# A two-layer trunk on one core: gate weights stacked as hi and lo, late constants moved, shift tiles in groups of four

## The chip, the core and the metric

The kernel runs on one core of a Trainium2 chip. Times are device microseconds of one execution; the time of a kernel is the median of its runs. The profile is of one further execution, recorded by the hardware profiler. PE is TensorE (PEld its weight loads), DVE VectorE, ACT ScalarE, POOL GpSimd, SP SyncE, whose queue issues most DMAs.

## The reference

One inference step of a two-layer trunk over 640 tokens (128 of context, 512 latent), width 2048, all in fp32. Each layer is an adaptive RMSNorm, an input projection, two mixers side by side, a SiLU gate, an output projection and a gated residual add. What the change touches is the modulation of the first layer and the low-rank gate of the linear attention:

```python
def modulation(cond, w, b):                    # cond: context vector, latent vector
    m = jax.nn.silu(cond) @ w + b              # w: 2048 x 6144
    return jnp.split(m, 3, axis=-1)            # shift, scale, gate

shift, scale, gate = modulation(c, ada_w[l], ada_b[l])
h = rms_norm(x, norm_g[l]) * (1.0 + scale) + shift
qa, ka, va, qb, kb, vb, rb, gp = split_cols(h @ w_in, EVEN_SPLITS)   # rb: 32 columns

r = rb.reshape(B, T, 2, GLA_RANK)              # gla_branch: two directions, rank 16
logit = jnp.einsum('btdr,drk->btdk', r, wg) + bg
g = jax.nn.log_sigmoid(logit) / GLA_NORMALIZER
```

## The kernel before

Tokens lie along the free dimension, features along the 128 partitions, so a projection's output chunk is 128 (or fewer) features by 640 tokens, made in two halves of 320 (322 with two extra columns, see below). Products in fp32 are made of rounded parts: every operand x is split into hi (rounded, by ScalarE) and lo = x - hi (by GpSimd), in the fast format fp32r, and a product is the sum of three matmuls, hi x hi, hi x lo, lo x hi (`mm_k`, recorded in `mm`, L393). `acth` and `actl` are the parts of the activations, `whi` and `wlo` those of the weights. A weight chunk is split in four units of 512 rows (4 slices of 128); the split weights lie in a ring of 2560 columns, the raw ones in four slots of `wraw`.

The order on the engines is fixed when the program is built: a planner (`Pace`) keeps its own clock for every engine and lets small tasks (generators, `tick`) fall in between the matmuls when its clock says that their inputs are there. Engines and queues then run in that order. So an edit at one place lays out anew the order of what follows.

**Start stage** (`start`). It makes the first layer's scale (16 tiles of 128 features) and shift (16 tiles) for two condition vectors, normalises x, and makes the first six weight chunks (`FIRST`) on the way: one over its whole depth ("lead") and five in windows of 2, 2, 4 and 8 slices, altogether 576 matmuls. A scale tile is a product of the condition vectors (`cond`, 32 columns, stationary) with 16 blocks of 128 x 128 of weights (`ada`, moving), four at a time side by side in the array, into four bands of 32 rows of one bank (L1360). ScalarE copies the bank out, one more matmul with `sel` adds the bands and turns the row into a column. The weights come in blocks of 512 KB on SyncE's queue into a ring of six (`NR`), two blocks to a tile; when a tile's matmuls are issued, its two slots are loaded anew.

Of the 16 shift tiles, eight (`BOTH`) are made in this way after the scale tiles. The other eight are sums on VectorE (`shifts`): rows of the transposed weights (`ada_s`, 256 KB a row quarter, five buffers `raw`) times a broadcast row of silu(c) (`crow_s`, from DRAM), a part of them offloaded to GpSimd and ScalarE (`prod`). When all are there, the shift is written into two extra columns of `acth` and `actl` (L1082, L1083), which later chunks carry along (322 columns), and TensorE transposes it (`tr`, L398) for a copy in DRAM.

At the very start, the loads are issued as follows: cT (the condition vectors) and then the weights on SyncE's queue; `small` (all small constants), the sink's logits and `crow` on ScalarE's. `crow` is passed through SiLU and written to DRAM as `crow_s`.

**The chunk behind the stage** is `w_rb`, the 32 columns of the gate's rank. Its raw weights are broadcast to three bands of 32 columns as they are split (M = 96), so that the result stands three times on 96 partitions, where `gla_rank` wants it as `r` (with the weights `wgs`, loaded from `gla_wgp`). It takes three products like any other chunk.

Of the kernel before, what the change touches and what calls it, by code (L numbers as in the profile page):

```python
# [19 lines left out]
KT = D // 128  # L20
# [27 lines left out]
BOTH = 8  # L48

# [168 lines left out]
class Core:  # L218
# [15 lines left out]
    ("gla_m1", 128),  # L234
    ("gla_mu", 128),
]


class Trunk:
# [9 lines left out]
    def __init__(self, tc, d, es):  # L249
# [29 lines left out]
        nc.sync.dma_start(self.cT, d["cT"])  # L279
        small = self.P([128, sum(w for _, w in SMALL)], "small")  # L280
        nc.scalar.dma_start(small, d["small"])
        at, c = 0, {}
        for name, w in SMALL:
            c[name] = small[:, at : at + w]
            at += w
# [6 lines left out]
        self.mu = c["gla_mu"].bitcast(U32)  # L292
        self.act(self.cT, self.cT, AF.Silu)
# [241 lines left out]
    def wstart(self, chunks, acts):  # L535
# [17 lines left out]
        self.both = {c for kind, x in acts if kind == "h" for c in x[:2]}  # L553
        seven = {c for kind, x in acts if kind == "s" for c in x}
        for kind, x in acts:
            if kind == "c" and x >= FIRST:
# [90 lines left out]
    def wpump(self, force=False):  # L647
# [113 lines left out]
    def units(self, c, k0, evac):  # L761

        p = []
        for k in range(k0, KT, 4):
# [10 lines left out]
            self.wdone((c, k, 0))  # L775

# [528 lines left out]
    def start(self):  # L1305
# [5 lines left out]
        with tc.tile_pool(name="su", bufs=1) as su:  # L1311
# [6 lines left out]
            rows = Ring([self.adas[:, 960 + 128 * i : 1088 + 128 * i] for i in range(3)])  # L1318
# [32 lines left out]
            def tiles():  # L1351
                for i in range(KT + BOTH):
                    ws = [ring[(2 * i + q) % NR].rearrange("p (a b) -> p a b", b=128) for q in range(2)]
                    yield from self.until(*ws)
                    self.now += 0.2
                    for j in range(16):
                        g = 32 * (j % 4)
                        o, c, w = pm[g : g + 32, 0:128], cond[:, j, :], ws[j // 8][:, j % 8, :]
                        self.pe(0.0575, o, c, w)
                        nc.tensor.matmul(o, c, w, start=j < 4, stop=j >= 12)  # L1360
                    self.now += 0.2
                    for q in range(2):
                        load(2 * i + q + NR)
                    yield
                    r = rows.next()
                    nc.scalar.activation(r, pm[:, 0:128], AF.Copy)
                    yield from self.until(r)
                    p = pcol.next()
                    self.mm(p, r, self.sel)
                    f = i if i < KT else i - BOTH  # L1370
                    x = self.adab[:, 0, f : f + 1]
                    if i >= KT:
                        nc.vector.tensor_scalar(self.sh0[:, :, f], p, x, None, ALU.add)
                        continue
                    x, g = self.b1[:, 0, f : f + 1], self.ng[:, 0, f : f + 1]
                    nc.vector.tensor_scalar(self.A[0][:, f, :], p, x, g, ALU.add, ALU.mult)
                    yield from self.wait(f"sq{f}")
                    self.act_mod(0, f, xs[f % NX], 0, T)
                    load_x(f + NX)
                    self.flags.add(f"act{f}")  # L1380
                self.flags.add("tiles")

            def shifts():
                raws = [self.t(su, [128, PIECE], "raw", bufs=self.NRAW) for _ in range(self.NRAW)]
                junk = self.adas[:, 1472 : 1472 + PIECE // 2].bitcast(BF16)
# [13 lines left out]

                for i in range(len(raws) - 1):  # L1400
# [84 lines left out]
            crow = self.adas[0:32, 1344:1472]  # L1485
# [8 lines left out]
            while lead or todo:  # L1494
# [11 lines left out]
                else:  # L1506
                    self.now += 0.2
            while self.tasks or self.low:
# [577 lines left out]
    def program(self):  # L2086
# [94 lines left out]
        add(d["w_rb"], 96, True, None, lazy("vt", rows=96, then=lambda x: self.spawn(self.gla_rank(x))))  # L2181
# [328 lines left out]
        with tc.manual_schedule():  # L2510
# [13 lines left out]
            for kind, x in acts:  # L2524
# [3 lines left out]
                elif kind == "s":  # L2528
                    self.spair(*x)
                elif kind == "k":  # L2530
# [105 lines left out]
def _consts():  # L2636
# [17 lines left out]
    return {"cos": c4, "sin": s4, "emask": em, "sel": sel, "gla_m1": m1, "gla_mu": mu}  # L2654
# [32 lines left out]
def _layout(i):  # L2687
# [20 lines left out]
    o["ada0"] = x.reshape(2, 8, 128, KT + BOTH, 128).transpose(3, 0, 2, 1, 4).reshape(-1, 128, 1024)  # L2708
# [29 lines left out]
    o["small"] = np.concatenate([o.pop(k).reshape(128, w) for k, w in SMALL], 1)  # L2738
# [37 lines left out]
```

## Time and profile before

| | |
|---|---|
| median of 3 runs | 2119.41 us (2116.44 to 2121.92) |
| profiled execution | 2118.93 us |
| its span, first to last instruction | 2117.1 us, granted TensorE clock 0.994 |
| TensorE busy | 2058.0 us (97%) |
| VectorE, ScalarE, GpSimd busy | 1320.0, 1071.2, 1285.1 us |
| moved by DMA | 341 MB, 161 GB/s over the span |
| start stage, to the first matmul of w_rb | 144.36 us |
| w_rb chunk | 144.36 to 158.48 us |

The span is that of the instructions; the profiled execution's own time is 1.8 us longer. A row of the timeline gives start, length, engine, line, operation, output and inputs, the shapes, how many instructions were merged, and in brackets the idle time before it with what ended it. An fp32 matmul leaves two records in the trace, an fp32r matmul one. Line numbers are those of the kernel before; L213 is the helper through which the vector engines' instructions go, L427 that of the DMAs on SyncE's queue.

### The profile page before, as it was taken

What the parts mean: (1) busy time and instruction counts of PE and PEld (TensorE: products, weight loads), DVE (VectorE), ACT (ScalarE), POOL (GpSimd) and SP (SyncE); (2) the same over time, 40 slices, a digit from 0 to 9 for tenths busy, and PEclk for the clock granted to TensorE, in tenths of its full rate; (3) what the DMA queues carried; (4) which work ended last, traced back from release to release, by engine and by line L of the source; (5) the groups of instructions that cost most, each with busy time, mean ns of one, the idle gap of its engine ahead of it and who ended that gap; (6) DMA issues with size and microseconds to landing.
All of it is one profiled execution on the core that took longest, in us unless ns stands there. A gap on an engine that the chain in (4) does not pass through costs nothing. (4 is left out here: it accounts for less than half of the span.)

```text
span 2117.1 us, 40263 instructions
## 1 busy us (share of the span) xinstructions
PE 2058.0 (97%) x14345; PEld 2003.7 (95%) x14345; DVE 1320.0 (62%) x3063; ACT 1071.2 (51%) x2471; POOL 1285.1 (61%) x1082
## 2 busy tenths in 40 slices
PE   7999999999999999999999999999999999999996
PEld 6899999999999999999999999999999999999995
DVE  4856686666556554988666878777454444465335
ACT  5645565454666665543564444444444544454433
POOL 4756564445545544888565656655555577668873
PEclk9999999999999999999999999999999999999998
DMA  9966343336464544576643455444322344354437
GB/s 363 398 226 189 121 158 107 111 119 197 130 206 150 150 136 145 187 229 219 213 130 105 136 160 159 143 139 149 94 81 90 108 139 130 124 202 132 128 95 248
DMA packets 193401, 341.23 MB, mean 161 GB/s; under 512 B 20944, under 2 KB 70192, under 8 KB 193200
## 3 DMA queue, kind: packets, MB, share of 16 engines
q1 hardware_dynamic: 191728, 337.10, 49.4%
q8 instruction: 112, 1.84, 0.4%
q10 hardware_dynamic: 1472, 1.56, 0.2%
q14 instruction: 89, 0.73, 0.1%
HBM read 304.08 MB, written 31.88 MB: 159 GB/s over the span
## 5 line engine op out<-in xcount | busy, mean ns | idle before, releaser
L393 PE MATMUL bank<-acth,whi 128*128 128x320 f32 (+2 forms) x3320 | 1021.5, 318 | 10.6 <-ACT bc L213 2.8
L393 PE MATMUL bank<-actl,whi 128*128 128x320 f32 (+2 forms) x3320 | 994.7, 310 | 3.7 <-DMA actl<-bl_dram 2.1
L393 PE MATMUL bank<-acth,wlo 128*128 128x320 f32 (+2 forms) x3320 | 994.5, 311 | 3.5 <-POOL wlo L213 3.5
L213 POOL TENSOR_TENSOR wlo<-wraw,whi 128x512 fp32r<-128x512 f32 (+1 forms) x452 | 573.6, 1281 | 412.1 <-ACT whi L213 329.8
L393 PEld LDWEIGHTS bank<-acth,whi 128*128 128x128 f32 (+1 forms) x3320 | 617.6, 189 | 20.9 <-ACT bc L213 3.9
L393 PEld LDWEIGHTS bank<-actl,whi 128*128 128x128 f32 (+1 forms) x3320 | 617.4, 189 | 6.9 <-DMA actl<-bl_dram 3.3
L393 PEld LDWEIGHTS bank<-acth,wlo 128*128 128x128 f32 (+1 forms) x3320 | 617.5, 189 | 5.1 <-POOL wlo L213 5.1
L213 POOL TENSOR_TENSOR wlo<-rs,whi 128x384 fp32r<-128x384 f32 x370 | 408.1, 1123 | 183.2 <-ACT whi L213 143.6
L213 ACT ACTIVATE whi<-wraw 128x512 fp32r<-128x512 f32 (+1 forms) x460 | 262.9, 588 | 93.2 <-PE bank L393 60.7
L393 PE MATMUL bank<-eh,wlo 128*128 128x322 f32 (+1 forms) x666 | 207.2, 311 | 2.7 <-POOL wlo L213 2.7
L393 PE MATMUL bank<-eh,whi 128*128 128x322 f32 (+1 forms) x666 | 209.3, 314 | 0.0
L393 PE MATMUL bank<-el,whi 128*128 128x322 f32 (+1 forms) x666 | 206.9, 311 | 0.0
L213 ACT ACTIVATE whi<-rs 128x384 fp32r<-128x384 f32 x370 | 182.0, 514 | 48.5 <-PE bank L393 41.7
L213 DVE TENSOR_TENSOR wraw<-rs 128x768 f32<-128x768 f32 x74 | 98.8, 1335 | 124.7 <-POOL wlo L213 69.9
L213 DVE CUSTOM_DVE_ANT_0 adas<-adas,bank,partg 128x256 bf16<-128x256 f32 (+1 forms) x290 | 156.2, 539 | 12.6 <-DMA adas<-ada_g 5.3
L213 POOL TENSOR_TENSOR prod<-adas,mixrow 128x512 f32<-128x512 f32 x85 | 111.5, 1321 | 70.4 <-ACT prod L213 48.5
L213 ACT ACTIVATE arena<-arena,bc 128x512 f32<-128x512 f32 (+4 forms) x211 | 106.4, 527 | 79.8 <-DVE arena L213 77.0
L393 PEld LDWEIGHTS bank<-eh,wlo 128*128 128x128 f32 x666 | 125.5, 189 | 3.9 <-POOL wlo L213 3.7
L393 PEld LDWEIGHTS bank<-eh,whi 128*128 128x128 f32 x666 | 125.7, 189 | 0.1
L393 PEld LDWEIGHTS bank<-el,whi 128*128 128x128 f32 x666 | 125.8, 189 | 0.0
L213 DVE CUSTOM_DVE_ANT_0 adas<-adas,bank,part 128x512 bf16<-128x512 f32 x151 | 112.4, 744 | 9.8 <-DMA adas<-ada 6.8
L213 ACT ACTIVATE arena<-Y 128x320 f32<-128x320 f32 (+1 forms) x76 | 38.9, 512 | 152.1 <-DVE Y L213 125.9
(218 smaller groups left out, 2480.1 us busy)
## 6 DMA issues: line engine op xcount, KB each, us to landing
wraw<-w_even SPq DMA_DIRECT2D x176, 256.0 KB, 3.4
adas<-ada_g SPq DMA_DIRECT2D x128, 256.0 KB, 3.7
adas<-ada SPq DMA_DIRECT2D x128, 256.0 KB, 3.8
rs<-w_odd SPq DMA_DIRECT2D x50, 384.0 KB, 3.3
wraw<-w_odd SPq DMA_DIRECT2D x74, 256.0 KB, 3.5
wraw<-w_out SPq DMA_DIRECT2D x64, 256.0 KB, 3.9
rs<-w_odd SPq DMA_DIRECT2D x50, 256.0 KB, 3.8
Y<-ada SPq DMA_DIRECT2D x24, 512.0 KB, 7.3
```

The lines of the kernel that those rows point to most:

```text
L213: return f(*args, **kw)
L393: self.nc.tensor.matmul(out, lhsT, rhs, start=start, stop=stop, **kw)
```

## The change

Three edits.

1. The chunk `w_rb` is split into one block of 64 columns, 32 of hi and 32 of lo, and a new function `quad` runs it: for each slice the block is multiplied by `acth` and by `actl` (two matmuls of 64 rows of output). The result is copied out of the bank by ScalarE into two buffers of `gt`; a task then multiplies it by a constant matrix `rep` (64 of 128 rows by 96 columns, fp32), which adds hi's and lo's parts and writes the sum to the three bands.
2. At the start: cT goes from SyncE's queue to ScalarE's, ahead of `small`. The constants `gla_m1`, `gla_mu` and the new `rep` leave `small` (420 columns, now 164) for a block `late` (352 columns), loaded at the end of the stage's matmuls together with the sink, on SyncE's queue. `crow` is loaded on SyncE's queue after the first scale tile, by a task of its own; `shifts` waits for it. The first tile's copy goes to VectorE.
3. The eight shift tiles on TensorE become two groups of four tiles: 16 matmuls of 512 columns for a group, in two batches of eight that each take four blocks of the ring; one copy by ScalarE, four matmuls with `sel`. The weights in DRAM are laid out accordingly; blocks and bytes stay the same.

In the changed program TensorE has 64 + 2 matmuls where w_rb had 96, and 32 of 512 columns where the shift tiles had 128 of 128.

```diff
+GROUPS = (*((f, 1) for f in range(KT)), *((f, 4) for f in range(KT, KT + BOTH, 4)))
...
-        nc.sync.dma_start(self.cT, d["cT"])
-        small = self.P([128, sum(w for _, w in SMALL)], "small")
-        nc.scalar.dma_start(small, d["small"])
+        nc.scalar.dma_start(self.cT, d["cT"])
+        for n, parts in (("small", SMALL), ("late", LATE)):
+            small, at = self.P([128, sum(w for _, w in parts)], n), 0
+            if n == "small":
+                nc.scalar.dma_start(small, d[n])
+            else:
+                self.late = small
...
-        if m < M:
-            raw = raw[:, :, None, :].to_broadcast([128, n, M // m, m])
-            hi, lo = (x.rearrange("p a (b c) -> p a b c", c=m) for x in hl)
+        if key[0] in self.stacked:
+            hl = hi
+            hi, lo = hl[:, :, :m], hl[:, :, m:]
...
+    def quad(self, c, parts):
+        _, M, shift, _, evac = self.chunks[c]
+        units = [(c, k, 0) for k in range(0, KT, 4)]
+        banks = [self.pj(), self.pj()]
+        for half, p in enumerate(banks):
+            cs = self.cols(half, shift)
+            n = cs.stop - cs.start
+            for u in units:
+                w = self.wget(u)
+                for j in range(4):
+                    for i, x in enumerate((self.ah, self.al)):
+                        k = u[1] + j
+                        self.mm(p[:M, :n], w[:, j, :], x[:, k, cs], start=k == i == 0, stop=k == KT - 1 and i == 1)
+                    if j % 2:
+                        self.tick()
+            self.nc.scalar.activation(parts[half][:M, :n], p[:M, :n], AF.Copy)
+            self.drop(p)
...
+        def work():
+            for half, x in enumerate(parts):
...
+                self.mm(p[:96, : x.shape[1]], self.rep[:M, :], x)
+                evac(*((None, p) if half else (p, None)))
...
             def tiles():
-                for i in range(KT + BOTH):
-                    ws = [ring[(2 * i + q) % NR].rearrange("p (a b) -> p a b", b=128) for q in range(2)]
+                at = 0
+                for i, n in GROUPS:
+                    m = 8 // n
+                    for b in range(0, 2 * n, 4):
+                        e = min(b + 4, 2 * n)
+                        ws = [ring[(at + q) % NR].rearrange("p (a b) -> p a b", b=128 * n) for q in range(e - b)]
+                        yield from self.until(*ws)
+                        for k in range(m * b, m * e):
+                            g = 32 * (k % 4)
+                            o, c, w = pm[g : g + 32, 0 : 128 * n], cond[:, k, :], ws[k // m - b][:, k % m, :]
+                            nc.tensor.matmul(o, c, w, start=k < 4, stop=k >= KT - 4)
+                        for q in range(e - b):
+                            load(at + q + NR)
+                        at += e - b
...
+                    if i == 0:
+                        nc.vector.tensor_copy(r, pm[:, : 128 * n])
+                    else:
+                        nc.scalar.activation(r, pm[:, : 128 * n], AF.Copy)
...
             def shifts():
...
+                yield from self.wait("crow")
...
-            nc.scalar.dma_start(self.sink, d["attn_sink"].partition_broadcast(128))
-            nc.scalar.dma_start(crow, d["crow"].rearrange("a (b c) -> (a b) c", c=128))
-            self.act(crow, crow, AF.Silu)
-            nc.scalar.dma_start(d["crow_s"].rearrange("a (b c) -> (a b) c", c=128), crow)
+            def rows0():
+                yield from self.wait("act0")
+                nc.sync.dma_start(crow, d["crow"].rearrange("a (b c) -> (a b) c", c=128))
+                yield 3.0
+                self.act(crow, crow, AF.Silu)
+                nc.scalar.dma_start(d["crow_s"].rearrange("a (b c) -> (a b) c", c=128), crow)
+                self.flags.add("crow")
+                yield
...
+            nc.sync.dma_start(self.late, d["late"])
+            nc.sync.dma_start(self.sink, d["attn_sink"].partition_broadcast(128))
...
-        add(d["w_rb"], 96, True, None, lazy("vt", rows=96, then=lambda x: self.spawn(self.gla_rank(x))))
+        add(d["w_rb"], 64, True, None, lazy("vt", rows=96, then=lambda x: self.spawn(self.gla_rank(x))))
+        acts.append(("q", acts.pop()[1]))
...
+    rep = np.tile(np.eye(32, dtype=f), (4, 3))
...
+    x = [x[:, :, f : f + n].reshape(2 * n, -1, 128, n * 128).transpose(0, 2, 1, 3) for f, n in GROUPS]
```

More of the change, by code (lines that the diff above doesn't have):

```diff
@@ L233 @@
     ("gmlp_gT", 8),
[L234 to L235 removed]
 ]
+LATE = [("gla_m1", 128), ("gla_mu", 128), ("rep", 96)]
 class Trunk:
@@ L775, in units @@
             self.wdone((c, k, 0))
+    def quad(self, c, parts):
[15 more added lines that the diff above has]
+            self.drop(p)
+        for u in units:
+            self.wdone(u)
+        def work():
+            for half, x in enumerate(parts):
+                cs = self.cols(half, shift)
+                x = x[:M, : cs.stop - cs.start]
+                yield from self.until(x)
+                yield from self.bank()
+                p = self.sm()
+                self.mm(p[:96, : x.shape[1]], self.rep[:M, :], x)
+                evac(*((None, p) if half else (p, None)))
+                yield
+        self.spawn(work(), first=True)
     @staticmethod
@@ L1317, in start @@
             sq, rt = self.adas[:, 0:T], self.adas[:, T : T + HT]
-            rows = Ring([self.adas[:, 960 + 128 * i : 1088 + 128 * i] for i in range(3)])
+            rows = Ring([self.adas[:, 960 + 512 * i : 1472 + 512 * i] for i in range(2)])
             NX, NR = 3, self.NRING
@@ L2529, in program @@
                     self.spair(*x)
+                elif kind == "q":
+                    self.quad(x, [L["gt"].next() for _ in range(2)])
                 elif kind == "k":
```

75 lines of the change are left out of this document (39 added, 36 removed).

## The prediction

> **What bounds the kernel now.** I read the page first, then busy time by stretches, then the timeline of the first 10 us and of 90 to 160 us, then the waits.
>
> ```profile
> span 2117.1 us, 40263 instructions
> PE 2058.0 (97%) x14345; PEld 2003.7 (95%) x14345; DVE 1320.0 (62%) x3063; ACT 1071.2 (51%) x2471; POOL 1285.1 (61%) x1082
> DMA  9966343336464544576643455444322344354437
> ```
> The profiled execution took 2118.93 us, 0.48 under the median of the runs (2119.41); 1.8 us of it lie outside the span. TensorE is busy nearly throughout, so a matmul less is time less, except where TensorE waits for data: the DMA row is full only in the first slices, that is in the start stage. The change is in that stage and in the chunk after it.
>
> ```profile
> 3.00:4.00 1.00, 0.00 (x0) 0.00 (x0) 0.30 (x1) 0.65 (x2) 0.46 (x5) 1.00 0.72 256
> 4.00:5.00 1.00, 0.00 (x0) 0.00 (x0) 0.32 (x1) 0.00 (x0) 0.29 (x4) 1.00 0.50 153
> 5.00:6.00 1.00, 0.00 (x0) 0.00 (x0) 0.00 (x0) 0.00 (x0) 0.00 (x0) 1.00 0.55 202
> ...
> 60.00:80.00 20.00, 20.00 (x259) 18.26 (x259) 16.82 (x29) 11.66 (x25) 16.59 (x12) 1.00 1.04 404
> 80.00:100.00 20.00, 19.22 (x242) 17.04 (x244) 15.93 (x33) 13.95 (x33) 10.17 (x8) 1.00 1.03 406
> 100.00:120.00 20.00, 18.02 (x237) 15.80 (x226) 10.55 (x30) 7.76 (x21) 11.95 (x10) 1.00 0.91 317
> 120.00:140.00 20.00, 20.00 (x139) 20.00 (x138) 16.84 (x50) 9.53 (x23) 14.33 (x12) 1.00 0.65 202
> 140.00:160.00 20.00, 20.00 (x139) 19.95 (x138) 6.44 (x19) 8.24 (x20) 10.89 (x12) 1.00 0.63 197
> ```
> Columns: length, busy time of PE, PEld, DVE, ACT, POOL, clock, DMA share, GB/s. From 60 to 100 us the transfers run at 405 GB/s, full, and TensorE is full as well: two bounds, side by side. From 3 to 6 us the transfers run at half that rate. From 120 us on TensorE is the only bound.
>
> ```profile
> 0.74 0.39 SPq L279 DMA_DIRECT2D cT<-cT  x1
> 1.18 0.45 ACTq L213 DMA_DIRECT2D sink<-attn_sink  x1
> 1.18 0.90 SPq L427 DMA_DIRECT2D Y<-ada  x2
> ...
> 3.44 0.23 ACT L213 ACTIVATE cT<-cT 128x32 f32<-128x32 f32 x1
> ...
> 3.54 0.29 POOL L213 TENSOR_SCALAR b<-small 128x32 f32<-128x32 f32 x1 [2.13 <-DMA small<-small]
> ...
> 6.62 1.08 PE L1360 MATMUL bank<-Y,cond 128*32 128x128 f32 x16 [6.62 <-DMA Y<-ada]
> ```
> The first matmul waits 6.62 us for the first block of modulation weights, issued at 1.18.
>
> ```profile
> 111.48 1.40 PE L1360 MATMUL bank<-more,cond 128*32 128x128 f32 x32
> 114.11 1.16 ACT L213 ACTIVATE bank<-raw 128x512 f32<-128x512 f32 x2 [3.15 <-DMA raw<-crow_s]
> 115.42 0.75 DVE L213 CUSTOM_DVE_ANT_0 adas<-raw,bank,sh 128x512 bf16<-128x512 f32 x1 [4.60 <-DMA raw<-ada_s]
> 138.84 0.08 DVE L213 DVE_READ_ACCUMULATOR2_ANT sh<- 128x1 f32 x1
> 139.79 0.28 DVE L213 TENSOR_TENSOR sh<-sh,small 128x8 f32<-128x8 f32 x2
> 141.61 0.27 PE L398 MATMUL bank<-ident,sh 128*32 128x128 f32 x1
> 144.36 0.31 PE L393 MATMUL bank<-acth,whi 128*96 128x322 f32 x1
> 158.48 0.31 PE L393 MATMUL bank<-acth,whi 128*128 128x322 f32 x1
> ```
> These are the stage's last steps: the last shift tile at 111.48, VectorE's sums of the other eight shifts from 115.42 to 140.07, the transposition of the shifts at 141.61, the gate-rank chunk (w_rb) from 144.36 to 158.48. From the last tile on TensorE has matmuls enough: what moves the start of w_rb moves the end.
>
> **The gate-rank chunk.** Before, 96 matmuls (16 slices of the depth, two halves, three products) take 14.12 us, 0.147 each. After, hi and lo stand side by side in 64 columns and two products do the work of three: 64 matmuls, 9.4 us. The moving side (322 or 320 columns) sets the pace, and it stays. So 4.7 us go. Two plain fp32 matmuls come, which add hi and lo and copy the sum into three bands. Their nearest row is another fp32 matmul of that width:
>
> ```profile
> 94.64 0.70 PE L393 MATMUL bank<-ssq,ones 128*128 128x320 f32 x2
> L393 PE MATMUL bank<-ssq,ones x4: 432/432/502, 89.3 to 94.9; 128*128 128x320 f32 x4
> ```
> One such matmul is two records that start 0.70 - 0.43 = 0.27 us apart: 0.54 us each, 1.1 for two. Net 3.6 us less; 3.2 if each costs 0.2 more for a change of the array's shape (row below). Splitting the weights gets cheaper on ScalarE and GpSimd (128 columns in place of 384), both off the path. New: all four weight blocks are wanted within the first half, 3.5 us after its start.
>
> ```profile
> 142.73 1.02 POOL L213 TENSOR_TENSOR wlo<-wraw,whi 128x384 fp32r<-128x384 f32 x1 [4.19 <-ACT whi L213]
> 147.36 0.42 ACT L213 ACTIVATE wgs<-arena 96x256 fp32r<-96x256 f32 x1 [3.14 <-DMA adas<-shift_s]
> 163.30 0.72 ACT L213 ACTIVATE r<-arena 96x640 fp32r<-96x640 f32 x1
> ```
> Before, the last one is split at 142.73, in time; had it the same time after, nothing waits, and each us later costs one. The late constants and the sink are now issued on SyncE's queue behind the next chunk's weights, ahead of the load that wgs waits for. Even 5.7 us more (the sink's landing, next part) puts wgs at 153, ahead of r at 163.30, where it is first needed: 0, with 10 us to spare.
>
> **The shift tiles.**
>
> ```profile
> 104.59 0.28 PE L393 MATMUL bank<-small,adas 128*128 128x2 f32 x2
> 104.80 1.08 PE L1360 MATMUL bank<-Y,cond 128*32 128x128 f32 x32
> 105.81 0.41 PE L393 MATMUL bank<-acth,whi 128*128 128x320 f32 x1
> 105.81 0.19 PEld L393 LDWEIGHTS bank<-acth,whi 128*128 128x128 f32 x1 [0.20 <-issue]
> ```
> A tile is 16 matmuls in 32 records, 1.01 us with 0.20 of idle array at its end, and 0.21 for its column matmul. Four tiles: 4.04. In a group, 16 matmuls of 512 columns stream the same number of columns: 4 x 0.81 = 3.24, with two ends of 0.20: 3.64. Two groups save 0.8 us of TensorE, 8 copies of ScalarE become 2. But a group is run in two batches that each wait for four blocks of 512 KB, so what counts is when these land.
>
> **First weights first.** The first weight block is issued at 0.74 in place of 1.18: 0.44 us. From 3 to 6 us 611 KB moved where 405 GB/s make 1215: 1.5 us lost, just while the sink's load was under way on ScalarE's queue:
>
> ```profile
> L213 ACTq DMA_DIRECT2D sink<-attn_sink x1: 449/449/449, 1.2 to 1.2; - x1
> ...
> DMA to landing us min/median/max: 5.7/5.7/5.7
> ```
> It is 4 KB, 32 bytes to each partition, and needs 5.7 us. That load and the one of crow leave the start; 131 KB of constants go too (0.3 us). The stream of weights so comes earlier by 0.44 to 2.3 us. I take 1.6, nearer the upper end, because the slow stretch ends when the sink lands.
> The Trainium skill (DMA: Bandwidth & Descriptors, Queues, rings and completion order) says that each DMA engine takes turns between the queues it has work for, a packet at a time. By that rule cT and the smaller constants, now both on ScalarE's queue, take the sink's place beside the first block; what that would give is a rival below. The trace agrees in so far as 153 GB/s go with two queues at work and 405 with one.
>
> Against this stands the order of SyncE's queue. Up to the last shift block it issues 41.70 MB before and 42.75 MB after (three more rows of ada_s and one weight block ahead of it): 1.05 MB, 2.6 us at 405 GB/s. Before, the last blocks landed about 112.2 (the last tile ran 1.40 where 1.08 is usual). After: 112.2 + 2.6 - 1.6 = 113.2 (112.5 to 114.4). In the changed program's order the last batch stands after 384 of the stage's 576 window matmuls. It ends 0.6 after its data, at 113.8; then 192 matmuls (28.2 us) and four column matmuls (0.8) lead to w_rb: 142.8. Data decide here, by little: the third batch's data end 3.41 MB (8.4 us) earlier in the queue, at 104.8, it ends at 105.2, and 48 matmuls (7.1) bring TensorE to the last batch at 112.3. What the earlier batches make it wait lies in front of that and costs nothing more.
>
> One wait is new. The transposition stands after 510 of the 576 matmuls, before after 558, so TensorE meets it at 113.8 + 126 x 0.147 + 0.8 = 133.1, and behind it on TensorE stand the last 66 matmuls and w_rb. VectorE's sums took 24.65 us from 115.42 (0.83 each with its read, and the adds of the windows). After, 22 sums remain where 24 did: 23.0 us. Their row of c comes 1.57 MB earlier in the queue, 3.9 us, and 1.6 with the stream: start at 109.9, end 132.9, and some 1.3 more because two blocks (1.05 MB, 2.6 us) land between the third and the fourth row: 134.2. TensorE waits 1.0 us (0 to 6.9, the latter if the sums end at 140.07 as before). So w_rb starts at 143.9 in place of 144.36: 0.5 less.
>
> ScalarE's wait at 114.11 goes with the earlier row of c, and with it this one of TensorE:
>
> ```profile
> PE bank L393 <- ACT adas L213: 1.8, 1, 1.8
> PE bank L393 <- POOL wlo L213: 6.2, 8, 1.4
> PE bank L398 <- ACT arena L213: 4.8, 8, 1.2
> ```
> The first row is of 60 to 118 us; the 1.8 are already in the count above, since data set the last batch. The other two are of the whole run. Behind w_rb the work is the same, but the order of the vector engines is laid out anew, so such waits can come out otherwise: half of these 11 us either way, +-5, with no sign.
>
> Sum: 2118.9 - 3.6 - 0.5 = 2114.8.
>
> **Rivals.**
> - The start gives all it can: the stream comes 2.3 us earlier, the sums finish before the transposition. Last data 112.5, w_rb at 142.1: 2118.9 - 3.6 - 2.3 = 2113.0, and some us less where later waits fall well. For it: the half-rate stretch ends with the sink. Chance 0.32.
> - ScalarE's queue still takes the first block's turns: 256 rows of cT and of the constants (128 each) stand there where the sink stood. The stream gains 0.44: last data 114.4, w_rb at 145.1 with the wait of 1.0: 2116.1. For it the rows of 3 to 6 us, against it that cT and the larger constants were both in by 3.5 us. Chance 0.14. It is the Trainium skill's rule of turns, from the page named above, by which the gain would be that of the issue alone.
> - The transposition becomes the wait: the sums end at 140.1, TensorE stands 6.9 us, and w_rb starts at 149.7: 2118.9 - 3.6 + 5.3 = 2120.6. Against it: the sums' data come earlier. Chance 0.12.
> - Slower: the ring of six blocks runs dry. A batch frees four blocks at once and only two are then under way. If the queue behind them is short, each refill shows its whole landing time:
>
> ```profile
> DMA to landing us min/median/max: 3.4/4.3/9.8
> ```
> That is of the 256 KB rows from 85 to 142 us. Three refills at 4.3 are 12.9 us: 2127.7. It decides once less than 1.7 MB (4.3 us) is queued when a batch ends. By the order, 1.83 MB stand behind the first batch's last block, so it is close but held. Chance 0.08.
>
> **How the numbers follow.** The forecast, 2114.8, has 0.34, with 2111 to 2119 as its own range. A measurement of this kernel tells 0.3% (6.4 us) from no change: bounds 2113.0 and 2125.8. Faster: three quarters of the first rival, 0.24, and 0.12 of the forecast's lower end, 0.36. Slower: the last rival and 0.01 of the transposition, 0.09. The same: 0.55. The range 2107 to 2122 leaves out the slow rival and the ends of the later waits.
>
> **What would show it.** Right: first tile matmul before 5.5 us, 153 to 256 GB/s of 3 to 6 us become about 400; w_rb from about 144 with 64 matmuls in 9.4 us; two 96-row fp32 matmuls at 0.54; TensorE's wait at the transposition near 1 us. Wrong: a first matmul still past 6 us; DMA shares under 0.9 between 80 and 110; w_rb starting past 147; waits of TensorE past 160 us that differ by more than 5 us in sum.

## The result and the profile after

The changed kernel takes 2135.11 us (median of 4 runs, 2132.37 to 2137.91), the kernel before in the same series 2120.36: a ratio of 1.0072, 95% interval 1.0055 to 1.0089. It is slower by 15.3 us (11.7 to 18.9), where 2114.8 was forecast and 2107 to 2122 given as the range. Its profiled execution took 2132.37 us.

The page of the changed kernel:

```profile
span 2130.6 us, 39826 instructions
PE 2057.7 (97%) x14125; PEld 2000.2 (94%) x14125; DVE 1309.8 (61%) x3051; ACT 1075.1 (50%) x2479; POOL 1293.9 (61%) x1090
...
DMA  9966343335465454476634444444322344363437
```
TensorE's busy time is 0.3 us less, although some 4 us of work went; and it stands idle 72.9 us (2130.6 - 2057.7) where it stood 59.1. So the span grew by waits, and what the removed work gave was eaten by matmuls that ran slower: the mean granted clock fell from 0.994 to 0.989.

Busy time by stretches of the changed kernel (length, busy time of PE, PEld, DVE, ACT, POOL, clock, DMA share, GB/s):

```profile
3.00:4.00 1.00, 0.00 (x0) 0.00 (x0) 0.00 (x0) 0.00 (x0) 0.00 (x0) 1.00 1.05 407
4.00:5.00 1.00, 0.00 (x0) 0.00 (x0) 0.05 (x1) 0.23 (x1) 0.00 (x0) 1.00 1.05 405
5.00:6.00 1.00, 0.81 (x16) 0.61 (x18) 0.14 (x1) 0.00 (x0) 0.00 (x0) 1.00 1.00 384
...
18.00:28.00 10.00, 5.77 (x47) 5.25 (x48) 2.07 (x5) 4.90 (x11) 4.75 (x4) 0.50 0.90 334
60.00:80.00 20.00, 16.41 (x204) 14.50 (x201) 16.12 (x34) 11.31 (x25) 15.80 (x12) 1.00 1.02 390
80.00:100.00 20.00, 18.39 (x195) 14.41 (x186) 13.87 (x28) 11.52 (x26) 12.91 (x10) 0.91 1.00 382
100.00:120.00 20.00, 20.00 (x135) 15.71 (x136) 10.12 (x26) 9.27 (x21) 7.85 (x7) 1.00 0.95 356
120.00:140.00 20.00, 19.12 (x134) 17.22 (x133) 15.84 (x47) 10.44 (x26) 15.99 (x13) 1.00 0.78 250
140.00:160.00 20.00, 20.00 (x138) 19.51 (x137) 6.16 (x20) 4.74 (x13) 9.01 (x12) 1.00 0.36 110
```
The first weights do come at full rate from 3 us on. But from 60 to 80 us TensorE is busy 16.4 us of 20 where it was busy all 20, and from 80 to 100 part of its work runs at a lower clock. Where that began is in the timeline of the changed kernel (start, duration, queue or engine, operation, and in brackets the wait and what ended it):

```profile
5.19 1.94 PE L1404 MATMUL bank<-Y,cond 128*32 128x128 f32 x32 [5.19 <-DVE cond L214]
...
13.06 0.34 SPq L1545 DMA_DIRECT2D Y<-crow  x1
...
20.56 0.31 ACT L214 ACTIVATE Y<-Y 32x128 f32<-32x128 f32 x1 [6.86 <-DMA Y<-crow]
...
21.92 0.26 ACT L214 ACTIVATE adas<-bank 128x128 f32<-128x128 f32 x1
...
22.23 0.59 PE L398 MATMUL bank<-small,adas 128*128 128x2 f32 x2 [7.70 <-ACT adas L214]
...
154.72 0.31 PE L398 MATMUL bank<-acth,whi 128*64 128x322 f32 x1
...
164.08 0.31 PE L398 MATMUL bank<-acth,whi 128*128 128x322 f32 x1
...
165.06 0.78 PE L398 MATMUL bank<-arena,late 64*96 64x322 f32 x2
...
168.57 0.41 ACT L214 ACTIVATE arena<-bank 64x320 f32<-64x320 f32 x1
...
169.04 0.78 PE L398 MATMUL bank<-arena,late 64*96 64x320 f32 x2 [2.11 <-ACT arena L214]
...
384.71 3.24 POOL L214 TENSOR_TENSOR prod<-adas,mixrow 128x512 f32<-128x512 f32 x2
385.06 1.77 DVE L214 TENSOR_TENSOR arena<-Y 128x640 f32<-128x640 f32 x1
386.75 1.88 DVE L214 TENSOR_TENSOR Y<-arena 128x640 f32<-128x640 f32 x1
388.56 0.81 DVE L214 TENSOR_TENSOR arena<-Y 128x640 f32<-128x640 f32 x1
...
390.16 0.47 PE L403 MATMUL bank<-ident,Y 128*128 128x128 f32 x1 [5.00 <-DVE Y L214]
390.29 0.61 PE L398 MATMUL bank<-acth,whi 128*128 128x320 f32 x1
390.70 0.47 PE L398 MATMUL bank<-actl,whi 128*128 128x320 f32 x1
390.97 0.47 PE L398 MATMUL bank<-acth,wlo 128*128 128x320 f32 x1
```
Four things are to be seen. First, crow's 16 KB were issued at 13.06 behind several blocks of weights on SyncE's queue; ScalarE takes its work in order, so its SiLU of crow waited 6.86 us, and the copy of the second tile's row stood behind it; TensorE waited 7.70 us. After that wait the clock was 0.50 from 18 to 28 us. Second, the gate-rank chunk started at 154.72, not at 144.36 as before, and its 64 matmuls took 9.36 us. Third, the second adding matmul waited 2.11 us, since the copy of its half stood in ScalarE's queue behind work that itself waited for GpSimd. Fourth, far behind the change, at 385, two VectorE operations took 1.8 us where the same operation takes 0.81 when GpSimd is not at work beside it; TensorE waited 5.00 us for their result, and its next matmuls started 0.27 us apart in place of 0.15.

### The profile page after: what moved, and what is told of

It is laid out like the page before. It is cut to its first block, busy times and chain, and to the rows that moved or that the text cites. A ratio compares the mean times of both kernels' runs of the same rounds, so it can differ in the third digit from the quotient of the medians.

```text
span 2130.6 us, 39826 instructions
## 1 busy us (share of the span) xinstructions
PE 2057.7 (97%) x14125; PEld 2000.2 (94%) x14125; DVE 1309.8 (61%) x3051; ACT 1075.1 (50%) x2479; POOL 1293.9 (61%) x1090
## 4 chain that ended last, share of the span: by engine, by line
PE 81%; DMA 6%; DVE 4%; POOL 3%; issue 3%; ACT 2%; SPq 1%; POOLq 0%; DVEq 0%; ACTq 0%
PE bank L398 79%; PE bank L403 2%; POOL wlo L214 2%; DVE Y L214 1%; DVE adas L214 1%; DMA Y<-xT 1%; DMA arena<-yT_dram 1%; DMA wraw<-w_even 1%; DVE arena L214 1%; DMA rs<-w_out 1%; POOL actl L214 1%; SPq L432 1%; DVE bank L214 0%; DMA actl<-bl_dram 0%; DMA raw<-crow_s 0%
## 5 line engine op out<-in xcount | busy, mean ns | idle before, releaser
L398 PE MATMUL bank<-acth,wlo 128*128 128x320 f32 (+1 forms) x3288 | 986.3, 311 | 2.4 <-POOL wlo L214 2.4
L398 PEld LDWEIGHTS bank<-acth,wlo 128*128 128x128 f32 x3288 | 614.4, 190 | 3.5 <-POOL wlo L214 3.4
L214 POOL TENSOR_TENSOR prod<-adas,mixrow 128x512 f32<-128x512 f32 x93 | 122.4, 1325 | 75.2 <-ACT prod L214 42.9
L214 DVE CUSTOM_DVE_ANT_0 adas<-adas,bank,part 128x512 bf16<-128x512 f32 x143 | 106.4, 744 | 18.4 <-DMA adas<-ada 12.3
L214 ACT ACTIVATE arena<-Y 128x320 f32<-128x320 f32 (+1 forms) x76 | 38.9, 512 | 147.8 <-DVE Y L214 118.7
```

What stands on the lines that cost most here:

```text
L214: return f(*args, **kw)
L398: self.nc.tensor.matmul(out, lhsT, rhs, start=start, stop=stop, **kw)
```

## The experiments

Ratios are to the kernel before, run beside each on the same chip, with a 95% interval; one hundredth of a per cent is 0.2 us. "Order" is the order of the instructions on an engine.

**1. Crow's load early.** It goes to ScalarE's queue at the start; the order of all engines stays that of the changed kernel.
```diff
-  nc.sync.dma_start(crow, d["crow"]...)      # in the task
+  nc.scalar.dma_start(crow, d["crow"]...)    # at the start
```


> The changed kernel with one line moved: the load of crow is issued on ScalarE's queue at the start, as before the change; its SiLU stays in its place, and every engine's order is that of the changed kernel. Theory A (the SiLU of crow holds ScalarE until a load that stands behind 7.5 us of weights on SyncE's queue, and TensorE waits 7.70 us for a copy behind it): that wait goes, w_rb starts at about 146 to 147 in place of 154.7, the time is 7 to 9 us below the changed kernel, 2126 to 2128. Rival B (the groups' four blocks set the stage's end whatever stands before): w_rb starts past 152, time within 3 us of the changed kernel. Rival C (the later waits are the cost): the start is mended but the time stays over 2130.


Measured 2133.15 us, 1.0055 (1.0037 to 1.0072). TensorE's wait near 14 us fell from 7.70 to 0.70, yet the kernel gained only some 2 to 4 us, within the overlap of the intervals, and the gate-rank chunk still started at 150.77. Crow's wait was real and was not the main cause: theory A's 2126 to 2128, with the chunk from 146 to 147, didn't come. The later waits (2.11, 5.01 and 2.73 us at 163, 384 and 818) stood as they were, as rival C has it.

**2. The same without the stacking:** 96 matmuls as before.
```diff
-  add(d["w_rb"], 64, ...); acts.append(("q", acts.pop()[1]))
+  add(d["w_rb"], 96, ...)
```


> As e1_crow_early, and the gate-rank chunk as before the change (96 matmuls, three products, no matrix rep). If stacking is worth the 3.6 us of the prediction, this is 2 to 5 us slower than e1_crow_early; if the wait for the copy ahead of the second rep matmul (2.11 us in the changed kernel) and the two rep matmuls eat it, within 1.5 us of it.


2126.43 us, 1.0027 (1.0015 to 1.0039). Without the part that was to save 3.6 us it is 6.7 us faster, where 2 to 5 us slower or no difference was expected. The wait at 388 us is 0.55, the one at 818 is gone.

**3. The first without the groups:** each shift tile by itself.
```diff
-  GROUPS = ... ((f, 4) for f in range(KT, KT + BOTH, 4))
+  GROUPS = tuple((f, 1) for f in range(KT + BOTH))
```


> As e1_crow_early, and the eight shift tiles one at a time as before the change. Theory A: within 2 us of e1_crow_early (the groups save 0.8 us of TensorE and move blocks about). Rival B (the groups' waits cost): 4 us or more faster than e1_crow_early, with w_rb starting that much earlier.


2136.03 us, 1.0077 (1.0062 to 1.0092), the chunk from 157.44 in place of 150.77: in this order the groups seem to help, by some 3 us, though the intervals of the two kernels overlap.

**4. The first with the sink's load early as well,** on ScalarE's queue.
```diff
-  nc.sync.dma_start(self.sink, ...)          # behind the windows
+  nc.scalar.dma_start(self.sink, ...)        # at the start
```


> As e1_crow_early, and the sink's load too back on ScalarE's queue at the start; every engine's order unchanged. If the sink's 128 pieces of 32 bytes slowed the first weight blocks, the first matmul starts at about 6.2 us in place of 5.2 and the second block's 1.5 to 2 us later than in e1_crow_early; the time is 0 to 2 us longer. If the slow stretch from 3 to 6 us has another cause, both start as in e1_crow_early within 0.4 us.


2130.39 us, 1.0052 (1.0033 to 1.0071): no difference to be told. From 3 to 6 us the weights came at 403, 411 and 372 GB/s with the sink early too, and the first matmul started at 5.13 us (5.08 without it). A slow stretch came from 6 to 8 us (148 and 327 GB/s). The trace's packet records put the sink's pieces of 32 bytes there, from 5.4 to 7.5 us; before, they ran from 2.9 to 6.6, across the slow stretch of 3 to 6. Yet with the sink late (1) the same two microseconds carry no more: 283 and 211 GB/s. So that the sink alone slowed the first weights is not borne out, and what did stays open.

**5. Each part alone.** Four kernels: the stacking, the groups, the start's edits, and groups with the start's edits but crow at its old place.
```diff
 # stacking alone, groups alone: the start as before
-  nc.scalar.dma_start(self.cT, d["cT"])
+  nc.sync.dma_start(self.cT, d["cT"])       # all constants, sink and crow early too
 # stacking alone, start alone: single tiles; groups alone, start alone: 96 matmuls
 # groups and start with crow back
-  self.spawn(rows0())
+  nc.scalar.dma_start(crow, ...); self.act(crow, crow, AF.Silu); ...   # at once
```


> The kernel before with one part of the change alone: the gate-rank weights' hi and lo side by side (64 matmuls and two fp32 ones in place of 96); tiles singly, the whole start as before. Theory S (stacking itself costs, because its second adding matmul waits behind ScalarE's queue and the planner lays out the work of the following hundreds of us anew): 2125 to 2128, as the pair with and without stacking was 6.7 us apart, with a wait of TensorE of 3 to 5 us near 375 to 385 us. Theory P (as predicted, the 32 matmuls less are worth 3.6 us and the later waits of the other kernels came from the start): 2117, no such wait.

> The kernel before with the groups of four shift tiles alone. Theory S (the parts add up; groups gave 2.9 us in the pair with and without them): 2117 to 2118, the gate-rank chunk starting about 142. Rival (a batch of four blocks frees the ring all at once and the stream stalls): 2123 to 2128, with DMA shares below 0.9 between 80 and 110 us and the chunk from 148 on.

> The kernel before with the start's edits alone: cT and small constants on ScalarE's queue, first weights first, late constants and the sink late, crow's load and SiLU in a task of their own after the first tile. Theory S (the start's edits are what makes the gate-rank chunk late; crow's wait is 2 us of it): 2128 to 2131, TensorE waiting about 7 us near 14 us and the gate-rank chunk from about 155. Rival (the groups in combination with the start make the late chunk): 2120 to 2123, the chunk from 146 to 148.

> Groups and the start's edits, but crow's load, SiLU and write in their old place at the start (no task, nothing waits for it, VectorE's copy of the first row back on ScalarE), and no stacking. Theory S1 (crow's task, by its place in the planner's order, is what makes the start's edits cost): 2114 to 2118, the gate-rank chunk starting at 141 to 144. Theory S2 (the order in which weights now come first makes it cost, crow or not): 2125 to 2127, as with crow's load alone moved back, and the chunk at 150 to 152.


Stacking 2131.79 us, 1.0065 (1.0051 to 1.0079). Groups 2126.05, 1.0032 (1.0020 to 1.0045). Start 2134.84, 1.0071 (1.0058 to 1.0083). Groups and start with crow back 2127.42, 1.0038 (1.0024 to 1.0052). Stacking, the start, and groups with the start came out slower than either theory had put them; groups alone took the time of its rival, but with DMA shares of 0.91 to 1.03 from 80 to 110 us the stream did not stall. Each part alone loses, and the three losses make 1.68%, not the 0.72% of the whole. So something common to all was in each; all four share the rewritten tile loop.

**6. The loop alone.** No part of the change; the tile loop as the changed kernel has it, with single tiles. It gives way to the planner once more per activation tile and moves the planner's clock 0.3 us more.
```diff
+                   self.now += 0.15                  # twice per tile
...
                        self.flags.add(f"act{f}")
+                       yield
```


> None of the three parts: tiles singly, start as before, 96 matmuls. Only the tile loop is written as in the changed kernel: it gives way once more to the planner after each of the 16 activation tiles, moves the planner's clock by 0.3 us more per tile, and has two row buffers where there were three. The work is that of before, the order differs on TensorE from its 112th instruction on. Theory N (this new order is what makes the start stage late in all variants run so far): 2125 to 2129, TensorE idle up to 160 us for 14 us or more where before it was 8.9. Rival (the order is harmless; each part costs by itself): 2119 to 2121.5.


2129.62 us, 1.0043 (1.0026 to 1.0060), just above the 2125 to 2129 of theory N: 9 us for the same matmuls in another order. Its busy time by stretches:
```profile
40.00:60.00 20.00, 15.38 (x155) 13.09 (x154) 12.11 (x26) 9.06 (x20) 9.76 (x7) 0.83 1.01 392
60.00:80.00 20.00, 19.34 (x227) 17.39 (x227) 16.39 (x38) 12.03 (x26) 13.87 (x10) 1.00 1.01 367
80.00:100.00 20.00, 17.13 (x200) 15.01 (x201) 13.93 (x31) 11.01 (x25) 11.06 (x8) 0.91 1.02 385
```
From 60 to 100 us TensorE is busy 36.5 us where it was busy 39.2 before, and part of that at a lower clock; the gate-rank chunk starts at 153.53. The order of TensorE differs from its 112th instruction on: 102 window matmuls stand ahead of the seventh tile's end where 84 stood.

**7. The loop giving way as before, with single tiles** (and 96 more columns of constants, as in 6). Each instruction stands where it stood before.
```diff
-                   self.now += 0.15
+                   self.now += 0.15 * (n > 1)
...
-                       yield
```


> The loop that can do groups, set to single tiles and giving way as before, with 96 more columns of constants in the start's load: each instruction stands where it stood before. Theory N (the order makes the difference): 2119 to 2121, the same as before. Rival (the 48 KB more at the start, or the two row buffers, delay the stage): 2124 or more.


2122.08 us, 1.0002 (0.9992 to 1.0011). The constants and the two row buffers cost nothing that can be told: what cost in 6 is the new lay-out. In the trace the chunk starts at 146.41, where the profiled execution of before, with the same order, had 144.36, and those of 11, with the same order up to there, 145.14 and 146.14: by so much the start of the chunk differs between executions.

**8. Groups with that loop, and groups with the start's transfers, crow at its old place.**
```diff
-  GROUPS = tuple((f, 1) for f in range(KT + BOTH))
+  GROUPS = ... ((f, 4) for f in range(KT, KT + BOTH, 4))
 # the second kernel, besides
-  nc.sync.dma_start(self.cT, d["cT"])
+  nc.scalar.dma_start(self.cT, d["cT"])     # and late constants and sink late
```


> Groups of four shift tiles, start as before, 96 matmuls, and the loop giving way and moving the planner's clock for single tiles as before: TensorE's first 561 instructions stand in the order of before. Theory N: 2116 to 2119, the groups giving the 2 to 3 us that the pair of runs with and without them gave, the gate-rank chunk from 141 to 143. Rival (groups cost by themselves): 2125 to 2127 as with the disturbed loop.

> The same with cT on ScalarE's queue, the first weights first and the late constants and the sink late; crow at its old place. The order of TensorE is that of the run beside it. Theory N: 2114 to 2118, 1.5 to 2 us under the run beside it, since the first tile's matmul comes at 5.1 where it came at 6.6. Rival (the ring is emptied by TensorE at a pace set elsewhere, and the early start is lost): as the run beside it within 0.7 us.


Groups 2122.59 us, 1.0014 (1.0004 to 1.0023), 3 us above before and not the 1 to 3 below that I expected. With the start 2121.16, 1.0004 (0.9995 to 1.0014), the same as before and above the 2114 to 2118 expected; it is 1.4 us under the run beside it, which the noise also allows. The windows do end early: in the second, TensorE reaches the transposition of the shifts at 141.1, and there it waits. Its timeline:
```profile
141.10 0.31 PE L398 MATMUL bank<-acth,wlo 128*128 128x320 f32 x1
144.89 0.40 PE L403 MATMUL bank<-ident,sh 128*32 128x128 f32 x1 [3.48 <-DVE sh L214]
145.15 0.58 PE L398 MATMUL bank<-acth,whi 128*96 128x322 f32 x1
145.53 0.47 PE L398 MATMUL bank<-actl,whi 128*96 128x322 f32 x1
145.80 0.47 PE L398 MATMUL bank<-acth,wlo 128*96 128x322 f32 x1
```
VectorE's sums ended only then: they had themselves waited 4.55 and 4.30 us for rows of ada_s, at 113 and 118 us. The gain of the groups turned into a wait of 3.48 us for them, and the wait cost more behind it: the gate-rank chunk's first matmuls start 0.27 us apart, so its first 64 take 11.8 us in place of 9.4.

**9. The start's transfers alone with that loop,** TensorE's and GpSimd's order that of before.
```diff
-  nc.sync.dma_start(self.cT, d["cT"])
+  nc.scalar.dma_start(self.cT, d["cT"])     # and late constants and sink late; single tiles
```


> Single tiles, TensorE's and GpSimd's order that of before; only the start's transfers differ: first weights first, cT and the smaller constants on ScalarE's queue, late constants and sink late. As predicted for this part: 1.5 to 1.8 us less, 2117.5 to 2118.5. Rival (the ring's pace is set by TensorE freeing its slots, the early start is lost later in the stage): 2119 to 2120.5.


2121.42 us, 1.0006 (0.9997 to 1.0014): nothing gained, and 1.5 us or more of gain is outside the interval. The column matmuls of the first and the third tile, in this kernel and then in 7:
```profile
9.45 0.58 PE L398 MATMUL bank<-small,adas 128*128 128x2 f32 x2 [2.25 <-ACT adas L214]
...
19.49 0.28 PE L398 MATMUL bank<-small,adas 128*128 128x2 f32 x2
```
```profile
10.83 0.59 PE L399 MATMUL bank<-small,adas 128*128 128x2 f32 x2 [1.86 <-ACT adas L214]
...
19.37 0.28 PE L399 MATMUL bank<-small,adas 128*128 128x2 f32 x2
```
A lead of 1.38 us at the first of these is gone 10 us later. Part of it went in the transfers: from 7 to 9 us this kernel's run at 279 and 291 GB/s, where those of 7 run at 399 and 424. What took the rest isn't settled.

**10. The stacking in the kernel before, its loop untouched.**
```diff
-  add(d["w_rb"], 96, ...)
+  add(d["w_rb"], 64, ...); acts.append(("q", acts.pop()[1]))   # with quad, as changed
```


> The kernel before, its loop untouched, with the side-by-side weights alone. Theory S (the stacking costs by itself): 2126 to 2128, with the waits of 5.0 us near 384 and 2.7 us near 819 us. Theory P (as predicted): 2117, without them. Theory N allows both; it says only that TensorE's idle time up to 140 us is that of before (within 1 us).


2124.20 us, 1.0021 (1.0012 to 1.0030), with waits of 5.01 us at 378 and 2.73 at 813 as in theory S, though 2 us under its time. It costs by itself; but is it the stacking, or the new order behind it?

**11. The planner's clock alone,** put back by 3.6 us and, in another kernel, put forward by 1.0 us behind the gate-rank chunk. TensorE's instructions are those of before. Those of the other engines nearly are: whether VectorE or GpSimd makes a product of the modulations' sums, the planner decides by the same clock (`offload`), and GpSimd makes 109 of them in both kernels where it made 104.
```diff
         self.units(c, 0, evac)
+        if self.chunks[c][1] == 96:
+            self.now -= 3.6                  # the other kernel: += 1.0
```


> The kernel before, with the planner's clock put back by 3.6 us after the gate-rank chunk, as if that chunk were shorter: the same instructions, in another order behind TensorE's 1288th. Theory R (any new lay-out of the later work costs): 2122 to 2126, with a wait of some us at 380 to 390 or 810 to 860 us. Rival (the stacking's waits are its own): 2118.5 to 2121, waits past 160 us in sum within 2 us of those of before (27).

> The kernel before, the planner's clock put forward by 1.0 us behind the gate-rank chunk: the same instructions in another order behind TensorE's 1288th. Theory R (a new lay-out of the later work loses, whatever its sign): 2124 to 2131. Rival (only a clock that runs ahead of the chip loses, since it then lets work in too early): 2119 to 2122.


Put back: 2131.55 us, 1.0050 (1.0038 to 1.0063), more than the 2122 to 2126 of theory R. Put forward: 2126.98, 1.0032 (1.0020 to 1.0045), as theory R has it. Either sign loses, with the same matmuls. The first one's timeline has the pattern of the changed kernel at another place:
```profile
305.11 1.80 DVE L213 TENSOR_TENSOR Y<-arena 128x640 f32<-128x640 f32 x1
306.83 1.88 DVE L213 TENSOR_TENSOR arena<-Y 128x640 f32<-128x640 f32 x1
308.64 2.15 DVE L213 TENSOR_TENSOR Y<-arena 128x640 f32<-128x640 f32 x1
...
307.99 6.29 POOL L213 TENSOR_TENSOR YB<-YB,rstd 128x640 f32<-128x640 f32 x3
...
310.84 0.48 PE L398 MATMUL bank<-ident,Y 128*128 128x128 f32 x1 [4.93 <-DVE Y L213]
```
VectorE's chain behind the gate's scan falls beside work of GpSimd, takes twice as long, and TensorE stands.

**12. All three parts with the loop of 7, crow at its old place.**
```diff
 # to the second kernel of 8
-  add(d["w_rb"], 96, ...)
+  add(d["w_rb"], 64, ...); acts.append(("q", acts.pop()[1]))
```


> All three parts, with the loop giving way as before and crow at its old place. Theory N: 2124 to 2127, that is 8 to 11 us less than the changed kernel, and 3 to 5 above the same without the stacking (2121.2), with the waits near 380 and 815 us. Rival (with groups and start in order the stacking gives what was predicted): 2117 to 2118.


2129.96 us, 1.0039 (1.0026 to 1.0052), above the 2124 to 2127 expected: 5 us under the changed kernel and 9 above the same without the stacking (8). TensorE waits 3.10 us at 160, 5.00 at 381 and 2.73 at 814.

**13. The stacking, planned with the time of 96 matmuls** and with the two halves taken in turn within each weight block.
```diff
 # in quad, to the kernel of 10
-  for half ...: for u in units: ...
+  for k0 in range(0, KT, 4): for half in range(2): ...
+      self.now += 0.148                       # per slice
```


> The kernel before with the side-by-side weights, the two halves of the tokens taken in turn within each weight block as before, and the planner told that each slice costs what three matmuls cost. Theory R: the later work is laid out anew all the same (the weight blocks are split and loaded at other points), so 2121 to 2130, with waits past 160 us of more than 30 in sum. Rival (the loss came from planning with the shorter chunk): 2117 to 2119, the 3.6 us less showing, waits past 160 us as before (27).


2136.29 us, 1.0083 (1.0069 to 1.0096), with waits of 5.00 us at 157, 4.05 at 387, 3.53 at 498 and at 827. That is slower than both theories had it; a plan that knows nothing of the saving does no better.

No version beats the kernel before; 7, the second kernel of 8, and 9 equal it.

## Why the prediction was wrong

**The step that failed** is the order, which the sum put at nothing. It stands in the prediction twice: "behind w_rb the work is the same, ... such waits can come out otherwise: half of these 11 us either way, +-5, with no sign", and for the start stage "what the earlier batches make it wait lies in front of that and costs nothing more". The span of the profiled execution came out 17.6 us above the one forecast (2130.6 against 2114.8 - 1.8). Of these, 10.8 lie ahead of the gate-rank chunk (154.72 against 143.9), none in it (9.36 against 9.4 us), and 6.8 behind it.

Two things lay the work out anew, the rewritten loop and whatever changes the planner's clock at the gate-rank chunk, and the 20 traces part by them. The columns give the start of the chunk, TensorE's waits past 160 us in sum (idle stretches over 0.15 us), and how many of the 68 VectorE operations of the form shown at 385 took over 1 us:

| | chunk from (us) | waits (us) | over 1 us | ratio |
|---|---|---|---|---|
| loop as before, clock as before (before, 7, 8, 9) | 144.4 to 147.4 | 26 to 30 | 24 to 26 | 1 to 1.0014 |
| loop as before, stacking or moved clock (10 to 13) | 145.1 to 147.7 | 34 to 38 | 30 to 34 | 1.0021 to 1.0083 |
| loop rewritten, no stacking (2, 6, three of 5) | 151.7 to 158.5 | 26 to 29 | 24 to 26 | 1.0027 to 1.0071 |
| loop rewritten, stacking (changed, 1, 3, 4, one of 5) | 150.1 to 157.4 | 33 to 35 | 29 to 30 | 1.0052 to 1.0077 |

So the loop makes the chunk late, and the stacking or a moved clock makes the later waits, with or without work taken away. I took a new order for a toss with a mean of nothing; all 15 kernels below the first row lost. Why the order of before is better than each of them isn't shown: it may have been picked among many, and no run tests that. Nor do the runs part the order behind the chunk from the products that the planner hands to GpSimd with it: 104 before, 105 in 13, 109 in 11, 111 to 114 in the other stacked kernels. The loop's loss doesn't hang on them: in 2 and in the start alone GpSimd made 104 as well.

In ratios, the loop's lay-out is 0.41% (6 against 7, 8.7 us); the stacking 0.22% on top of it (5 against 6, 4.7 us); the groups give 0.11% back (2.3 us); crow's wait is 0.17% (changed kernel against 1, 3.6 us). These make 14.7 of the 15.3 us; each carries some 4 us of uncertainty, so that is a plausible account and no proof to the microsecond.

**"W_rb starts at 143.9"** was out by 10.8 us: 154.72. The sum took the last batch's data as deciding and the matmuls ahead of it as covered. The batch stood where I had it, behind 384 window matmuls, but it ran from 122.4 to 124.4, where I had it done at 113.8, and it waited for no data: TensorE itself came late, after waits throughout the stage. From there to the chunk the sum held (30.3 us against 30.1). With the loop undisturbed (second kernel of 8) the batch ended at 118.7 and TensorE had its windows done at 141.4, ahead of the 142.8 of the sum; there VectorE's sums decided. I had them end at 134.2; they ended near 144.8, and near 144.6 in the changed kernel.

**Crow's load** I looked for only in what it freed at the start. Its new place on SyncE's queue, behind weights, and ScalarE's in-order queue behind its SiLU are the wait that the prediction didn't name: 7.70 us on TensorE, of which the total showed 2 to 4.

**First weights first:** the first matmul at 5.19 us and 384 to 407 GB/s from 3 to 6 us are as predicted; the sink as the cause of the slow stretch isn't borne out (4). The first matmul now waits for cT, by way of cond, and no longer for weights. The rival of turns between the queues (0.14) isn't borne out either: the transfers ran at that rate while cT and the constants were still landing on ScalarE's queue, until about 4.6 and 6.2 us. That the stream so stays early by 1.6 us is wrong (9): the time is unchanged.

**The gate-rank chunk:** 64 matmuls took 9.36 us, forecast 9.4. An adding matmul's two records span 0.78 us, a little more than the matmul I took them from (0.70), and the first held TensorE from 165.06 to 165.77, 0.71 us where I had 0.54; the 2.11 us in front of the second are what was left out, the queue of its half's copy on ScalarE. Of 3.6 us less on paper nothing reached the end: every pair with and without it went the other way, by 4.5 to 9 us, and by 17.6 in 13. wgs came at 160.59, later than the 153 that I allowed, and still ahead of its use.

**The groups:** 3 us in 1 against 3, and 2.3 in 5 against 6, both in a late order and within the noise of a pair; where the start is in order, their rival came true. "The transposition becomes the wait" (chance 0.12, priced at 6.9 us) is what stands there in 8, with 3.48 us. In the changed kernel itself it was covered, since TensorE came to it only at 144.92.

**The ring running dry** didn't happen: DMA shares of 1.00 and 0.95 from 80 to 120 us.

## What to carry to other kernels

Where a program's order is laid out by a planner, first run the planner's change without the change of work: here a moved clock alone cost 0.3 to 0.5%, more than the 0.2% forecast for the edit. Then keep the order of everything the edit doesn't touch, and compare orders ahead of comparing times. A wait of TensorE is to be priced with the slower matmuls behind it, and a small load moved to a busy queue with the in-order engine that waits for it.

## What the runs showed of the hardware

**The clock behind a wait.** In the 20 traces of this case, take TensorE's waits that began between 20 and 2050 us, and ask whether a stretch at a granted clock of 0.50 began between the wait's start and 4 us after its end. All 19 waits of 3 us or more had one; of those of 2 to 3 us 27 of 42, of those of 1.2 to 2 us 34 of 129. A stretch lasts 3.4 us or a multiple; matmuls then start 0.267 us apart in place of 0.147, which makes 1.5 us lost for each (3.4 x (1 - 0.147 / 0.267)). The changed kernel has eight such stretches ahead of the last one at its end, the kernel before three. The Trainium skill (TensorE: Matmul & The Clock Gate, Why this matters for your kernels) advises against idle gaps above about 3 us; the traces agree, and show that shorter ones are often punished too.

**VectorE beside GpSimd.** The same operation on 128 x 640 values of fp32 took 0.81 us alone and 1.77 to 2.15 beside GpSimd's work. GpSimd's two products at 385 took 1.44 and 1.84 us where one alone takes 1.29:

```profile
L214 POOL TENSOR_TENSOR prod<-adas,mixrow x2: 1442/1642/1842, 384.7 to 386.1; 128x512 f32<-128x512 f32 x2
```
The ends tell how they meet: GpSimd's first product ends at 386.15, VectorE's operation at 386.83 (0.68 later), GpSimd's second at 387.95 (1.12 later), VectorE's next at 388.63 (0.68 later). Each ends a little less than its own time (0.81 or 1.29) behind the other's end, so the two take turns, and both look slow because each waits for the other. The Trainium skill (SBUF — State Buffer, SBUF: two separate sides) says that the two engines share a pair of ports and that the loser is blocked for the whole instruction of the other; the trace agrees. The planner reckons with this exclusion too (`lock` in `Pace.record`), but on its own clock; in the kernels with later waits more of VectorE's operations are slow (table above).
